# Attention probabilities turned by VectorE and a round trip through HBM in three of four key groups, on one Trainium2 core

## The chip, the core and the metric

The kernel runs on one core of a Trainium2 chip. A core has five engines with a queue of instructions each: TensorE (PE) multiplies matrices, VectorE (DVE) and ScalarE (ACT) work on elements, GpSimd (POOL) does a little arithmetic and issues some of the transfers, SyncE (SP) issues the rest. Each engine takes its instructions strictly in order; semaphores hold an instruction until what it needs is done. Working memory (SBUF) and the accumulators of the matrix engine (PSUM) have 128 partitions each. Data and weights lie in HBM and are moved by 16 DMA engines that all queues share.

The metric is the device time of one execution in microseconds (us); smaller is better. All data is float32.

## The reference

One sequence of 256 tokens goes through one Mamba-2 layer and one layer of sliding-window attention; both add to the residual stream and normalise. The change lies in the attention layer alone: 32 query heads of width 64 share 4 key and value heads, so 8 query heads belong to one key group. A query sees the 128 latest keys, and a sink per head takes part in the softmax.

```
s = einsum("bcqhrd,bckhd->bchrqk", qb, kk) * (hd ** -0.5)
s = where((diff >= 0) & (diff < WINDOW) & (kpos >= 0), s, -inf)
m = maximum(max(s, axis=-1), sk)
p = exp(s - m)
p = p / (sum(p, axis=-1) + exp(sk - m))
o = einsum("bchrqk,bckhd->bcqhrd", p, vv)
o = o * silu(gate)
return o @ w_out
```

Queries lie on the partitions when the softmax is taken over keys. The product with the values contracts over keys, so the keys must then lie on the partitions: the probabilities have to be turned in between.

## The kernel before

**Weights.** All weights stream in once, in units of 128 x 2048. Each half of a unit (512 KB) is loaded by SP (L152), cast by ScalarE to a high part `wh` (L161), and VectorE takes the low part `wl` as the difference (L164). Every product is the sum of three matmuls, high by high, low by high and high by low. A unit keeps TensorE busy for some 5.5 us. Units are split two ahead of the one in use (`AHEAD`), in four buffers each for `wh` and `wl`.

**The attention layer** runs in the order of `B_ORDER`: for the four key groups j, a block of queries ("q", four units, L973), of gates ("g", four units, L249) and of the output projection ("o", four units, L320 to L322), as q0 g0 q1 g1 o0 q2 g2 o1 q3 g3 o2 o3. After each unit `tick()` counts down a list of delayed steps; `later(n, step)` puts a step n units ahead. So the small steps of attention stand between the units of the large products. A scheduler then orders the instructions within each engine's queue by its own estimate; what it made of both kernels is shown below.

**Attention of one group** has two passes, h = 0 for the first 128 queries and h = 1 for the second. `attend(j, h)`: scores on TensorE (L1090, L1097) into the PSUM tiles `ax` (there are four of them, which all small steps share); masks by VectorE into `p` (L1104, L1114); maximum (L1121); exponentials on ScalarE, a head at a time (L1127); scaling by the reciprocal of the sum (L1132). `turn_p`, three or four units later: eight transposes of 128 x 128 on TensorE (L1140; each shows as an instruction of its own), and copies out of PSUM into `pt` (L1149, L1151), which for h = 1 also multiply by the two masks that part the keys of the own block and the block before (L1144). `pv`: product with the values (L1161 for h = 0; L1178 and L1185 for h = 1), gating by VectorE into `o` (L1164, L1191), and the split of `o` into `oH` (ScalarE, L1200) and `oL` (VectorE, L1201), which the projection "o" of that group reads. The turns of the queries (`qtr`, L1051) take two `ax` tiles per group one unit after the block "q".

**Queues.** POOL's queue holds, in this stage, the loads of bias rows (L948), of rows for the residual (L1020), and at its end three normalisations.

Of the kernel before, what the change touches and what calls it, by code (L numbers as in the profile page):

```python
# [8 lines left out]
F32 = mybir.dt.float32  # L9
# [8 lines left out]
P = 128  # L18
# [41 lines left out]
NPT = 6  # L60
# [21 lines left out]
def trunk(ctx: ExitStack, tc: tile.TileContext, A: dict, out: bass.AP, dbg=None):  # L82
# [816 lines left out]
    def turn_x1(h, c, tp, tag, bufs):  # L899
# [8 lines left out]
        x1 = tp.tile([P, 512], F32, tag=tag, name=nm("x1"), bufs=bufs)[:].rearrange("p (k t) -> p k t", k=4)  # L908
# [37 lines left out]
    def bias_row(src):  # L946
        t = bp.tile([P, 512], F32, tag="bias", name=nm("bias"), bufs=2)
        nc.gpsimd.dma_start(t[:], src.partition_broadcast(P))  # L948
        return t
# [34 lines left out]
    for h in range(2):  # L984
        ps = mm_tile()
        for ui in range(4):
# [6 lines left out]
            if h == 0:  # L993
                for c in ((), (), (0, 1, 2, 3), ())[ui]:
                    turn_x1(1, c, bp, "pt", NPT)
# [80 lines left out]
    def attend(j, h):  # L1076


        nk = P * (h + 1)
        q2 = qT[j, h]  # L1080
        p = bp.tile([P, 8, P], F32, tag=f"p{h}", name=nm("p"), bufs=1)
        per = 512 // nk
        for b in range(0, 4, per):
# [17 lines left out]
            for par in range(2):  # L1101
                v = p[:, par * 4 + b : par * 4 + b + per, :]
                if h == 0:
                    nc.vector.tensor_tensor(  # L1104
                        v, pss[par][:].rearrange("p (a k) -> p a k", a=per),
                        mask_a0.unsqueeze(1).to_broadcast([P, per, P]), ALU.add,
                    )
                    continue
                got = pss[par][:].rearrange("p (a k) -> p a k", a=per)

                nc.scalar.copy(v, got[:, :, 64:192])
                for part, m, at in ((0, mask_own, 192), (1, mask_a0[:, 64:], 0)):
                    qs = slice(64 * part, 64 * part + 64)
                    nc.vector.copy_predicated(  # L1114
                        v[qs, :, qs], m[qs].bitcast(U32).unsqueeze(1).to_broadcast([64, per, 64]),
                        got[qs, :, at : at + 64],
# [4 lines left out]
        nc.vector.tensor_reduce(mx, p[:], AX.X, ALU.max)  # L1121
# [4 lines left out]
        for r in range(8):  # L1126
            nc.scalar.activation(  # L1127
                p[:, r, :], p[:, r, :], AF.Exp, bias=ng[:, r : r + 1], accum_out=rs[:, r : r + 1]
# [3 lines left out]
        nc.vector.tensor_tensor(p[:], p[:], ri.unsqueeze(2).to_broadcast([P, 8, P]), ALU.mult)  # L1132

        pts = {}

        def turn_p():
            for par in range(2):
                pt = ax_tile() if h else mm_tile()
                for a in range(4):
                    nc.tensor.transpose(pt[:, a * P : (a + 1) * P], p[:, par * 4 + a, :], ident)  # L1140
                for kc in range(h + 1):
                    t = bp.tile([P, 512], F32, tag="pt", name=nm("pt"), bufs=NPT)
                    if h:
                        nc.vector.tensor_tensor(  # L1144
                            t[:].rearrange("p (a q) -> p a q", a=4), pt[:].rearrange("p (a q) -> p a q", a=4),
# [257 lines left out]
```

## Time and profile before

| what | value |
|---|---|
| median of 3 runs | 993.49 us (993.34 to 993.56) |
| the profiled execution's own time | 993.77 us |
| its span, first to last instruction | 991.8 us |
| TensorE busy | 985.8 us (99%) |
| VectorE busy | 775.2 us (78%) |
| ScalarE busy | 566.5 us (57%) |
| GpSimd busy | 105.4 us (11%) |
| granted TensorE clock | 1.0 |
| first scores of attention (L1090) | at 720.6 us of the span |

A row of the timeline reads: start in us from the beginning of the span, busy time, engine, line, instruction, out<-in, shapes, how many instructions were merged into the row, and in brackets how long the engine had idled before it and what released it. TensorE is pipelined: an instruction's busy time is its time from entry to end, and the next one enters long before that end. What an instruction takes from TensorE's time is therefore the distance from its start to the start of the next row, not its busy time. A row of the view of waits reads: waiting instruction <- what it waited for: us in total, how many times, the longest. In the view of groups the columns behind the bar are the busy time in total, and the mean in ns of one instruction.

### The profile page before, as it was taken

To read this page: it belongs to the slowest core of one execution; us is meant where nothing else is said; L and a number is where in the kernel's file an instruction comes from. 1 tells how busy PE (TensorE), PEld (TensorE's weight loads), DVE (VectorE), ACT (ScalarE), POOL (GpSimd) and SP (SyncE) were. 2 spreads that over 40 slices of the span, in tenths; PEclk is the share of its full clock that TensorE was granted. 3 is DMA by queue.
4 is the path that set the end of the run, shared out by engine and by line. 5 is a ranking of instruction groups with operands and counts; after the bars stand their busy time and mean duration, and the time that the engine had idled before them with its cause. 6 is when DMAs were issued, how large, how long until landed. Compare 5 with 4: busy or idle time off the path is not lost.

```text
span 991.8 us, 18106 instructions
## 1 busy us (share of the span) xinstructions
PE 985.8 (99%) x7132; PEld 897.4 (90%) x7132; DVE 775.2 (78%) x1206; ACT 566.5 (57%) x992; POOL 105.4 (11%) x130
## 2 busy tenths in 40 slices
PE   9999999999999999999999999999999999999997
PEld 8999989999999998999999999888998978978976
DVE  7888897877786887686787687889688786686696
ACT  7585866547646654664664664566455544544542
POOL 0000303004003002100300300303100000000003
PEclk9999999999999999999999999999999999999999
DMA  9688577575576666656657466456754646456432
GB/s 363 241 270 328 164 262 223 172 236 176 193 232 187 219 207 196 208 180 209 208 170 236 139 203 215 157 178 223 253 185 154 192 159 197 158 159 196 158 128 86
DMA packets 61557, 198.90 MB, mean 201 GB/s; under 512 B 6848, under 2 KB 11360, under 8 KB 61216
## 3 DMA queue, kind: packets, MB, share of 16 engines
q1 hardware_dynamic: 58528, 188.53, 57.8%
q0 software_dynamic: 2336, 8.69, 2.7%
q8 instruction: 56, 0.92, 0.4%
q10 hardware_dynamic: 608, 0.52, 0.2%
q14 instruction: 29, 0.24, 0.1%
HBM read 195.49 MB, written 2.23 MB: 199 GB/s over the span
## 4 chain that ended last, share of the span: by engine, by line
PE 99%; DVE 0%; DVEq 0%; issue 0%
PE mm L249 53%; PE mm L973 11%; PE mm L320 9%; PE mm L321 9%; PE mm L322 9%; PE ax L628 2%; PE ax L604 1%; PE ax L1097 1%; PE ax L1090 0%; PE ax L587 0%; PE mm L387 0%; PE ax L1161 0%; PE ax L1140 0%; PE ax L1051 0%; PE ax L1178 0%; PE mm L1140 0%
## 5 line engine op out<-in xcount | busy, mean ns | idle before, releaser
L164 DVE TENSOR_TENSOR wl<-wr,wh 128x1024 fp32r<-128x1024 f32 (+2 forms) x338 | 393.1, 1182 | 103.6 <-ACT wh L161 101.5
L161 ACT ACTIVATE wh<-wr 128x1024 fp32r<-128x1024 f32 (+2 forms) x338 | 332.1, 1010 | 193.4 <-issue 69.1
L249 PE MATMUL mm<-xH,wh 128*128 128x256 f32 x1280 | 355.4, 278 | 0.0
L249 PE MATMUL mm<-xL,wh 128*128 128x256 f32 x1280 | 354.0, 277 | 0.0
L249 PE MATMUL mm<-xH,wl 128*128 128x256 f32 x1280 | 353.9, 277 | 0.0
L249 PEld LDWEIGHTS mm<-xH,wh 128*128 128x128 f32 x1280 | 240.4, 188 | 1.9 <-issue 0.5
L249 PEld LDWEIGHTS mm<-xL,wh 128*128 128x128 f32 x1280 | 240.6, 188 | 1.0
L249 PEld LDWEIGHTS mm<-xH,wl 128*128 128x128 f32 x1280 | 240.5, 188 | 0.2 <-DVE wl L164 0.2
L320 PE MATMUL mm<-wh,yH 128*128 128x512 f32 x256 | 101.4, 396 | 0.0
L321 PE MATMUL mm<-wh,yL 128*128 128x512 f32 x256 | 99.8, 390 | 0.0
L322 PE MATMUL mm<-wl,yH 128*128 128x512 f32 x256 | 99.7, 389 | 0.0
L644 POOL TENSOR_TENSOR yz<-yz,z 128x256 f32<-128x256 f32 x32 | 32.8, 1033 | 468.9 <-DVE yz L639 468.9
L249 PE MATMUL mm<-x1H,wh 128*128 128x256 f32 x256 | 71.7, 280 | 0.0
L491 DVE SCALAR_TENSOR_TENSOR cv<-mm,pc,cv 128x255 f32<-128x255 f32 x144 | 68.6, 477 | 3.3 <-ACT cv L489 1.9
L249 PE MATMUL mm<-x1L,wh 128*128 128x256 f32 x256 | 70.8, 277 | 0.0
L249 PE MATMUL mm<-x1H,wl 128*128 128x256 f32 x256 | 70.8, 276 | 0.0
L973 PE MATMUL mm<-wh,x1H 128*128 128x512 f32 x160 | 62.9, 393 | 0.0
L973 PE MATMUL mm<-wl,x1H 128*128 128x512 f32 x160 | 61.8, 389 | 0.0
L973 PE MATMUL mm<-wh,x1L 128*128 128x512 f32 x160 | 60.9, 389 | 0.0
L320 PEld LDWEIGHTS mm<-wh,yH 128*128 128x128 f32 x256 | 48.1, 188 | 10.3 <-DVE z L580 0.9
L322 PEld LDWEIGHTS mm<-wl,yH 128*128 128x128 f32 x256 | 48.0, 188 | 10.2
L321 PEld LDWEIGHTS mm<-wh,yL 128*128 128x128 f32 x256 | 48.1, 188 | 9.0
(226 smaller groups left out, 1346.8 us busy)
## 6 DMA issues: line engine op xcount, KB each, us to landing
wr<-in_wa SPq DMA_DIRECT2D x154, 512.0 KB, 5.0
wr<-in_wo SPq DMA_DIRECT2D x64, 512.0 KB, 4.4
wr<-in_wq SPq DMA_DIRECT2D x32, 512.0 KB, 4.5
wr<-in_wg SPq DMA_DIRECT2D x31, 512.0 KB, 4.7
wr<-in_wb SPq DMA_DIRECT2D x16, 512.0 KB, 4.1
wr<-in_wb SPq DMA_DIRECT2D x32, 256.0 KB, 3.7
rb<-rscr SPq DMA_DIRECT2D x11, 512.0 KB, 4.1
wr<-in_wkv SPq DMA_DIRECT2D x8, 512.0 KB, 4.9
```

Of the source, the lines that this page charges most:

```text
L161: m = nc.scalar.activation(h[:, sl], v, AF.Copy)
L164: m = nc.vector.tensor_tensor(l[:, sl], v, h[:, sl].bitcast(F32), ALU.subtract)
L249: m = nc.tensor.matmul(ps, a, b, start=first and i == 0, stop=last and i == 2)
L320: pinned(nc.tensor.matmul(ps, aH[:, k, hs], u.h[:, ks], start=k == 0 and add is None, stop=False), pin)
L321: pinned(nc.tensor.matmul(ps, aL[:, k, hs], u.h[:, ks], start=False, stop=False), pin)
L322: pinned(nc.tensor.matmul(ps, aH[:, k, hs], u.l[:, ks], start=False, stop=k == 3), pin)
L491: nc.vector.scalar_tensor_tensor(a[:, sft:], ps[:, : S - sft], w(3 - sft), a[:, sft:], ALU.mult, ALU.add)
L604: nc.tensor.transpose(ps[:, o : o + P], st.xs[i][:, c * P : (c + 1) * P], ident)
L628: nc.tensor.matmul(ps[64 * r : 64 * r + 64, cols], xd[:, c, r, :], e[:, 256:] if c else e[:, :256], start=c == 0, stop=c == 1,)
L644: nc.gpsimd.tensor_tensor(v, v, st.z[i][:], ALU.mult)
L973: m = nc.tensor.matmul(ps[:], (x1H, x1L, x1H)[i][:, kk, hs], (u.h, u.h, u.l)[i][:, ks], start=(kk, i) == (0, 0), stop=ui == 3 and (k, i) = ...
L1097: nc.tensor.matmul(pss[par][qs, at : at + 192], q2[rows, b + i, qs], kT[rows, j, 64 * part : 64 * part + 192], start=True, stop=True,)
```

## The change

In the groups j = 0, 1 and 2 (`far`) TensorE no longer turns the probabilities. `p` is laid out with the 32-wide blocks of keys outermost. VectorE transposes each block of 32 x 32 in place in the grid (one instruction over 128 x 1024, into a tile `z`), POOL stores `z` to HBM (512 KB), and when that has landed four more transfers (128 KB each, in runs of 1 KB) bring the blocks back to the partitions where they belong, into `pt`. For h = 1 VectorE multiplies by the two masks five units later, now in two instructions of 128 x 1024 from SBUF. The product with the values comes later: nine units after the first pass's `attend` in group 0 and eleven in the groups 1 and 2, and the two passes' products fall on the same unit. The group j = 3 still turns on TensorE.

Around it: the factor 0.5 goes from the gating into one more instruction on the reciprocals (128 x 8) in all groups; `o` shares the two buffers of the queries before their turn (tag "qt"); `p` and `z` share three buffers; `pt` has three buffers of 1024 for six of 512; the bias rows have one buffer for two; the tiles of the LayerNorm at both ends of the layer follow the new sizes.

```diff
@@ def attend(j, h):
-        p = bp.tile([P, 8, P], F32, tag=f"p{h}", name=nm("p"), bufs=1)
+        p = bp.tile([P, 1024], F32, tag="p", name=nm("p"), bufs=3)
+        far = j < 3
+        byhead = p[:].rearrange("p (c r b) -> p r c b" if far else "p (r c b) -> p r c b", r=8, c=4)
...
-        nc.vector.tensor_tensor(p[:], p[:], ri.unsqueeze(2).to_broadcast([P, 8, P]), ALU.mult)
+        nc.vector.tensor_scalar(ri, ri, 0.5, None, ALU.mult)
+        nc.vector.tensor_tensor(
+            byhead, byhead, ri.unsqueeze(2).unsqueeze(3).to_broadcast([P, 8, 4, 32]), ALU.mult
+        )
...
+        def turn_far():
+
+            z = bp.tile([P, 1024], F32, tag="p", name=nm("z"), bufs=3)
+            nc.vector.transpose(z[:], p[:])
+            zd = dram.tile([P, 1024], F32, tag="zd", name=nm("zd"), bufs=2)
+            nc.gpsimd.dma_start(zd[:], z[:])
+            t = pt_tile(0)
+            for c in range(4):
+                nc.gpsimd.dma_start(
+                    pts[0][32 * c : 32 * c + 32].rearrange("b i r a -> b i (r a)"),
+                    zd[:, c * 256 : (c + 1) * 256].rearrange("(i b) f -> b i f", b=32),
+                )
+
+            def parts():
+                own = pt_tile(1)
+                nc.vector.tensor_tensor(own, t, masked(1, 8), ALU.mult)
+                nc.vector.tensor_tensor(t, t, masked(0, 8), ALU.mult)
+
+            if h:
+                later(5, parts)
...
-            o = bp.tile([P, 4, P], F32, tag="o", name=nm("o"), bufs=1)
+            o = bp.tile([P, 4, P], F32, tag="qt", name=nm("o"), bufs=2)
...
-                nc.vector.scalar_tensor_tensor(
-                    o[:], ov[:].rearrange("p (a t) -> p a t", a=4), 0.5, sg[j][:, :, hs], ALU.mult, ALU.mult
-                )
+                gated(ov[:], 0, P)
...
-        last = j == 3
-        later(4 if last and h == 0 else 3, turn_p)
-        later((5 if last else 6) if h == 0 else (8 if 0 < j < 3 else 4), pv)
+        if not far:
+            later(3 + (h == 0), turn_p)
+            later(5 - h, pv)
+        else:
+            turn_far()
+            later((11 if j else 9) - 3 * h, pv)
         if h == 0:
-            later(1 if last else 3, lambda: attend(j, 1))
+            later(1 if j == 3 else 3, lambda: attend(j, 1))
```

**TensorE, group 1, at the end of the first unit of gates of group 2.** Before, this is what stood between that unit and the next: the product of the second pass with the values (`vt`), then the two turns of the queries `qt`, each into an `ax` tile of its own.

```order
L1178 MATMUL ax_9494<-pt_9256,vt 64x256
L1178 MATMUL ax_9494<-pt_9265,vt 64x256
L1178 MATMUL ax_9495<-pt_9258,vt 64x256
L1178 MATMUL ax_9495<-pt_9267,vt 64x256
L1185 MATMUL ax_9494<-pt_9258,vt 64x256
L1185 MATMUL ax_9495<-pt_9256,vt 64x256
L1185 MATMUL ax_9494<-pt_9267,vt 64x256
L1185 MATMUL ax_9495<-pt_9265,vt 64x256
L1051 MATMUL ax_9508<-cc,qt_9413 128x128 x4
L1051 MATMUL ax_9515<-cc,qt_9422 128x128 x4
```

Now, at the same place, both passes' products stand there (L1216 for the first, L1230 and L1237 for the second), and the second turn of the queries comes six matmuls of the next unit (L248) later.

```order
L1216 MATMUL ax_9467<-pt_8872,vt 64x512 x2
L1230 MATMUL ax_9474<-pt_9118,vt 64x256 x2
L1230 MATMUL ax_9475<-pt_9309,vt 64x256 x2
L1237 MATMUL ax_9474<-pt_9309,vt 64x256
L1237 MATMUL ax_9475<-pt_9118,vt 64x256
...
L1052 MATMUL ax_9488<-cc,qt_9384 128x128 x4
L248 MATMUL mm_9516<-x1H,wh_9348 128x256
...
L248 MATMUL mm_9516<-x1H,wl_9349 128x256
L1052 MATMUL ax_9495<-cc,qt_9393 128x128 x4
```

Five `ax` tiles are asked for in a row where there are four: `ax_9495` takes the place of `ax_9467`, once VectorE has read that. Group 2 has the same rows.

**VectorE, group 0, the second pass.** Before, the stretch from the product of the first pass (`o_8673`) to the next unit's split held the copies out of PSUM; L164 is the split of weights.

```order
L1164 SCALAR_TENSOR_TENSOR o_8673<-ax_8674,sg_8156 128x512
L1144 TENSOR_TENSOR pt_8687<-ax_8682,cc 128x512
L1144 TENSOR_TENSOR pt_8689<-ax_8682,cc 128x512
L1201 TENSOR_TENSOR oL_8679<-o_8673,oH_8678 128x4x128
L1144 TENSOR_TENSOR pt_8696<-ax_8691,cc 128x512
L1144 TENSOR_TENSOR pt_8698<-ax_8691,cc 128x512
```

Now the masks (L1168, L1169) stand one unit later between the halves of a split, and wait for the four loads of `pt_8556`.

```order
L163 TENSOR_TENSOR wl_8774<-wr_8777,wh_8773 128x1024
L163 TENSOR_TENSOR wl_8880<-wr_8881,wh_8879 128x1024
L1168 TENSOR_TENSOR pt_8834<-pt_8556,cc 128x8x4x32
L1073 SCALAR_TENSOR_TENSOR sg_8695<-sg_8695,mm_8708 128x256
L1169 TENSOR_TENSOR pt_8556<-pt_8556,cc 128x8x4x32
L163 TENSOR_TENSOR wl_8880<-wr_8883,wh_8879 128x1024
L163 TENSOR_TENSOR wl_8965<-wr_8966,wh_8964 128x1024
```

The gating and the split of `o` have left this stretch: they stand behind the softmax of group 1 now, as the next rows show.

```order
L1204 TENSOR_TENSOR o_8940<-ax_8941,sg_8154 128x512
...
L1245 TENSOR_TENSOR oL_8939<-o_8940,oH_8938 128x4x128
L1139 TENSOR_TENSOR p_8837<-p_8837,sm_8850 128x8x4x32
L1204 TENSOR_TENSOR o_8947<-ax_8948,sg_8154 128x4x64
L1156 STREAM_TRANSPOSE z_8868<-p_8837 128x1024
L1204 TENSOR_TENSOR o_8947<-ax_8949,sg_8154 128x4x64
L1073 SCALAR_TENSOR_TENSOR sg_8695<-sg_8695,mm_8889 128x256
L163 TENSOR_TENSOR wl_9026<-wr_9027,wh_9025 128x1024
L1245 TENSOR_TENSOR oL_8939<-o_8947,oH_8938 128x4x128
```

The last row (`oL` of the second pass) is what the second half of the first output unit of group 0 reads.

**POOL, group 0.** Before, only small loads stood in this part of the queue; now it reads as follows.

```order
L947 DMA bias_8459<-in_qb 128x512
L1158 DMA zd_8326<-z_8324 128x1024
L1161 DMA pt_8328<-zd_8326 32x4x256 x4
L1021 DMA gb_1062_8633<-in_lng 128x512
L1021 DMA gb_1063_8635<-in_lnb 128x512
L1158 DMA zd_8554<-z_8552 128x1024
L1161 DMA pt_8556<-zd_8554 32x4x256 x4
L947 DMA bias_9239<-in_qb 128x512
```

The last two loads for the residual (`gb`) now stand behind the first pass's round trip, and the queries' bias of group 1 ahead of it.

More of the change, by code (lines that the diff above doesn't have):

```diff
@@ L946, in bias_row @@
     def bias_row(src):
-        t = bp.tile([P, 512], F32, tag="bias", name=nm("bias"), bufs=2)
+        t = bp.tile([P, 512], F32, tag="bias", name=nm("bias"), bufs=1)
         nc.gpsimd.dma_start(t[:], src.partition_broadcast(P))
@@ L1178, in pv @@
                         nc.tensor.matmul(
-                            ovs[part][64 * par : 64 * par + 64], vt[:, part, vs], pt_of(part, par, whole, part),
+                            into(part, par), vt[:, part, vs], pt_of(part, par, whole, 2 * part, 2 * part + 2),
                             start=True, stop=False,
```

102 lines of the change are left out of this document (58 added, 44 removed).

## The prediction

> **What bounds the kernel now.** I read the page first (busy times, slices, the chain that ended last), then the view of waits for the attention layer (690 to 960 us), then TensorE's timeline around the instructions that go.
>
> ```profile
> PE 985.8 (99%) x7132; PEld 897.4 (90%) x7132; DVE 775.2 (78%) x1206; ACT 566.5 (57%) x992; POOL 105.4 (11%) x130
> PEclk9999999999999999999999999999999999999999
> PE 99%; DVE 0%; DVEq 0%; issue 0%
> ```
>
> TensorE is the whole chain, at the full granted clock. So an instruction taken from its queue is worth its pitch (start to next start), unless a new wait on that queue eats it.
>
> ```profile
> DVE wl L164 <- ACT wh L161: 33.0, 20, 4.2
> PEld ax L1140 <- ACT wh L161: 2.4, 3, 0.8
> PEld ax L1161 <- issue: 1.4, 4, 0.4
> PEld ax L1051 <- issue: 1.2, 3, 0.4
> ```
>
> In 270 us of attention nothing holds TensorE's queue for more than 0.8 us at a time, and VectorE still has waits of its own; DVE and ACT are cover, not bound.
>
> **1. The transposes that go.** Six groups of eight, of these the first and the last after a block of weights and the first and the last after a product with the values, each with the row behind it:
>
> ```profile
> 738.22 1.04 PE L1140 MATMUL mm<-cc,p 128*128 128x128 f32 x8
> 739.19 1.53 PE L1097 MATMUL ax<-kT,qT 64*64 64x192 f32 x32
> ...
> 758.22 1.09 PE L1140 MATMUL ax<-cc,p 128*128 128x128 f32 x8
> 759.07 0.37 PE L249 MATMUL mm<-x1H,wh 128*128 128x256 f32 x1
> ...
> 864.37 1.03 PE L1140 MATMUL mm<-cc,p 128*128 128x128 f32 x8
> 865.33 0.88 PE L1097 MATMUL ax<-kT,qT 64*64 64x192 f32 x16
> ...
> 884.36 1.09 PE L1140 MATMUL ax<-cc,p 128*128 128x128 f32 x8
> 885.21 0.49 PE L973 MATMUL mm<-wh,x1H 128*128 128x512 f32 x1
> ```
>
> Start to next start they take 0.97, 0.85, 0.96 and 0.85 us; group 1 is like group 2. Sum 0.97 + 2 x 0.96 + 3 x 0.85 = 5.44 us off TensorE. [...]
>
> **2. Both products on one unit.** Group 3 has the form that the groups 0 to 2 get; before, those have the products apart.
>
> ```profile
> 952.75 1.08 PE L1161 MATMUL ax<-pt,vt 128*64 128x512 f32 x4
> 953.66 1.03 PE L1178 MATMUL ax<-pt,vt 128*64 128x256 f32 x8
> 954.62 0.66 PE L1185 MATMUL ax<-pt,vt 64*64 64x256 f32 x8
> 955.21 0.50 PE L320 MATMUL mm<-wh,oH 128*128 128x512 f32 x1
> ...
> 809.06 0.39 PE L322 MATMUL mm<-wl,oH 128*128 128x512 f32 x1
> 809.38 1.08 PE L1161 MATMUL ax<-pt,vt 128*64 128x512 f32 x4
> 810.39 1.09 PE L1140 MATMUL ax<-cc,p 128*128 128x128 f32 x8
> ...
> 838.48 0.28 PE L249 MATMUL mm<-x1H,wl 128*128 128x256 f32 x1
> 838.69 1.08 PE L1178 MATMUL ax<-pt,vt 128*64 128x256 f32 x8
> 840.30 1.09 PE L1051 MATMUL ax<-cc,qt 128*128 128x128 f32 x8
> 841.14 0.36 PE L249 MATMUL mm<-x1H,wh 128*128 128x256 f32 x1
> 841.34 0.28 PE L249 MATMUL mm<-x1L,wh 128*128 128x256 f32 x1
> ```
>
> Together 955.21 - 952.75 = 2.46; apart 1.01 + 1.61 = 2.62; and the separate entry at 809.06 cost 0.32 for a pitch of 0.23. Saved: 3 x (0.16 + 0.09) = 0.75 us. Against it, in the groups 1 and 2 the second turn of the queries gets an entry and an exit of its own, 0.21 + 0.20 for two pitches of 0.12: 2 x 0.17 = 0.35 us back. TensorE's work so falls by 5.44 + 0.75 - 0.35 = 5.85 us.
>
> **3. A new wait, in the groups 1 and 2.** After the change the second turn of the queries needs the `ax` tile of the first product, and so VectorE's gating; the gating writes into a buffer of "qt" and so needs the first turn done. Before, VectorE and ScalarE do this at that place:
>
> ```profile
> 838.68 1.06 ACT L161 ACTIVATE wh<-wr 128x1024 fp32r<-128x1024 f32 x1 [3.41 <-PE mm L249]
> 839.91 1.05 ACT L161 ACTIVATE wh<-wr 128x1024 fp32r<-128x1024 f32 x1
> 839.77 1.23 DVE L164 TENSOR_TENSOR wl<-wr,wh 128x1024 fp32r<-128x1024 f32 x1 [2.59 <-ACT wh L161]
> 840.91 0.75 DVE L1191 SCALAR_TENSOR_TENSOR o<-ax,sg 128x256 f32<-128x256 f32 x2
> ```
>
> Count from T, the start of the products (838.69 here). VectorE: half a split at T + 1.08 (1.14 to the next row), the gate's 0.33, the other half of the split, ahead of the gating in the new order, then the gating of 128 x 512 (0.68, as L1164's like): begun at 1.08 + 1.14 + 0.33 + 1.14 = T + 3.69, done at T + 4.4. TensorE: products 2.46, half of 0.84 for the first turn, six matmuls at 0.12 with an exit 0.9: T + 3.8. It waits 0.7 us with the hand-over. Bounds: 0, if the gating goes ahead of the half split; 0.7 + 1.14 = 1.8, if one more half split stands ahead. I take 0.7, since the order and the rows give it: 1.4 us in both. Behind that wait stand 42 matmuls of a unit; VectorE for its part waits in the second gating for that turn, with a split queued behind, but units are split two ahead, some 10 us.
>
> **4. VectorE, ScalarE and the 32 x 32 transposes.** No row shows that instruction. Nearest below is a pass over the same tile, 1.22 us; above, two such passes, 2.44.
>
> ```profile
> L1132 DVE TENSOR_TENSOR p<-p,sm 128x1024 f32<-128x1024 f32 x8 | 9.8, 1219 | 0.1
> L1144 DVE TENSOR_TENSOR pt<-ax,cc 128x512 f32<-128x512 f32 x16 | 10.1, 680 | 0.0
> ```
>
> I take 1.22 (one pass in, one out, like L1132). Per group two transposes (2.4), two masks from SBUF at 1.22 for four at 0.68 (-0.3), a copy less (-0.7; and one less on ScalarE), the small factor twice (0.3): some +1.8 us on VectorE per 74 us, free under a TensorE that is the bound. The laying out of `p` in blocks I cost at nothing; its cover is VectorE's idle time. [...]
>
> **5. The round trip, and group 0.** Nearest rows for a store and a load from POOL, with POOL's time for issuing one:
>
> ```profile
> rb<-rscr POOLq DMA_DIRECT2D x5, 512.0 KB, 7.6
> el<-rscr POOLq DMA_DIRECT2D x2, 256.0 KB, 3.6
> DMA to landing us min/median/max: 3.4/5.3/8.8
> L1020 POOL DMA_DIRECT2D gb<-in_lnb x4: 536/538/538, 663.7 to 739.9; - x4
> L1003 POOL COPY kd<-kd x2: 1414/4014/6613, 679.3 to 688.7; 128x256 f32<-128x256 f32 x2
> ```
>
> (The row of landings is that of `rb`.) Store 5 us, then four issues of 0.54 of which three lie ahead of the last load, and 4 to 5 us for that: about 11 us. Bounds: 3.4 + 1.6 + 3.4 = 8.4, and 8.8 + 1.6 + 8.8 = 19.2 us. In the groups 1 and 2 some 15 us lie between the transpose and the masks (two and a half units of gates and queries), in all groups more than that before the products. Group 0 is the tight one:
>
> ```profile
> 751.62 1.22 DVE L1132 TENSOR_TENSOR p<-p,sm 128x1024 f32<-128x1024 f32 x1
> 764.71 1.06 ACT L161 ACTIVATE wh<-wr 128x1024 fp32r<-128x1024 f32 x1 [2.33 <-PE mm L249]
> 784.92 0.40 PE L320 MATMUL mm<-wh,oH 128*128 128x512 f32 x1
> ```
>
> The scaling ends 0.8 us earlier than here (852.84 less 100: 752.0; the turn of 0.97 ahead of it is gone), half a split follows, then the transpose: 754.2. VectorE reaches the masks behind a half split whose cast waits for TensorE (764.71, now 2.9 us earlier) and at the end of its own backlog: 765.1. That leaves 10.9 us, as much as the trip takes. From there VectorE runs masks, splits, the softmax of group 1, both gatings and one transpose to `oL` of the second pass at about 785.0; TensorE, 2.1 us earlier than before, begins the output unit at 782.8 and asks for that `oL` half a unit later, at 785.5. A lateness of the loads beyond 0.5 us is paid in full; I put 0.3 us for it.
>
> **The sum.** 5.85 - 1.4 - 0.3 = 4.15 us off. The profiled execution took 993.77 us, 0.28 above the median of the runs; it would take 989.6, and the median 993.49 goes to 989.3. I say 989.4 us. The tail (group 3) is costed at nothing: its transposes keep their places, and the two small factors (0.17 each, as L1123's like) lie under TensorE's units.
>
> **The rivals.** A difference under 0.2% (2 us) cannot be told from no change here.
>
> *No new wait.* VectorE gets to the gating before the half split, or the fifth tile is free: 993.49 - 5.85 = 987.6. For it: no wait of TensorE above 0.8 us now. Against: the order puts the split ahead. Chance 0.22.
>
> *Late in group 0.* The trip takes some 14 us (512 KB at 7.6, loads at 5): 3 us beyond the margin, all on TensorE: 992.3, no difference that can be told. For it: the `rb` row; weights share the DMA engines. Against: the rows of 256 KB. With the transposes at 2.44 us it is half as bad. Chance 0.17.
>
> *Slower: POOL's transfers are starved.* The masks stand in VectorE's queue in front of the splits. A trip of 19.2 us (the upper bound) is 8.3 us over the 10.9, of which 0.5 are free, 7.8 fall on TensorE in group 0, and about 4 over the 15 us in the groups 1 and 2, which VectorE's idle time there takes up: 993.49 - 4.45 + 7.8 = 996.8. It decides from a trip of 18 us on. For it: a POOL copy of the same shape took 1.4 us and 6.6 us, so something can hold POOL while VectorE works. Against: eight issues of the residual's rows, in the same traffic, took 536 to 538 ns each. [...] Chance 0.12.
>
> **How the numbers follow.** My forecast has 0.45, and 0.04 remain for what I have not seen. Faster by over 0.2% (under 991.5): 0.45 + 0.22 + 0.05 of the late case and the rest = 0.72; within: 0.16; slower: 0.12. The forecast's own range is 988.4 to 990.6 (its waits halved or doubled). The range for 8 in 10 runs from 987.3 (no wait) to 993.0 (late in group 0).
>
> **What would show it.** Right: TensorE's chain still 99%, 16 rows of transposes instead of 64, the two turns of the queries 0.7 us apart from waiting, VectorE's masks in group 0 with a wait of 0 to 1 us for the loads, the transposes at 1.2 us. Wrong: waits of TensorE at the first output unit of group 0, waits of VectorE for loads above 3 us, POOL issues much over 0.54 us, or block-wise passes over `p` well above 1.22 us.

## The result, and the profile after

| | before | after |
|---|---|---|
| median of 14 runs | 993.48 us (992.77 to 994.35) | 993.87 us (991.60 to 995.06) |
| ratio of after to before | | 1.0001, 95% interval 0.9993 to 1.0010 |
| the profiled execution | 993.77 us, span 991.8 | 995.06 us, span 992.9 |
| keys' turn to the tail (below) | 285.98 us | 286.95 us |

No difference that can be told, where 989.4 was forecast. The profiled execution of after is the slowest of its 14, so the trace shows somewhat more loss than the median has.

The page after: busy times, and the chain that ended last.

```profile
PE 982.9 (99%) x7084; PEld 893.7 (90%) x7084; DVE 780.8 (79%) x1211; ACT 565.1 (57%) x989; POOL 122.8 (12%) x160
PE 87%; DMA 5%; DVE 4%; ACT 1%; issue 1%; POOL 0%; ACTq 0%; SPq 0%; DVEq 0%; POOLq 0%
```

The 48 transposes are gone (7132 to 7084 instructions), but the chain is no longer TensorE alone: 5% transfers and 4% VectorE stand in it. TensorE's timeline shows where it loses time in the attention layer.

```profile
697.53 1.03 PE L1009 MATMUL ax<-cc,kd 128*128 128x128 f32 x8
...
762.29 0.60 PE L1052 MATMUL ax<-cc,qt 128*128 128x128 f32 x4
764.34 0.63 PE L1052 MATMUL ax<-cc,qt 128*128 128x128 f32 x4 [1.45 <-DVE qt L962]
764.72 0.36 PE L248 MATMUL mm<-x1H,wh 128*128 128x256 f32 x1
...
785.36 0.50 PE L319 MATMUL mm<-wh,oH 128*128 128x512 f32 x1
786.09 0.50 PE L320 MATMUL mm<-wh,oL 128*128 128x512 f32 x1 [0.23 <-DVE oL L1245]
...
788.52 0.40 PE L321 MATMUL mm<-wl,oH 128*128 128x512 f32 x1
789.68 0.50 PE L319 MATMUL mm<-wh,oH 128*128 128x512 f32 x1 [0.76 <-ACT oH L1244]
791.08 0.50 PE L320 MATMUL mm<-wh,oL 128*128 128x512 f32 x1 [0.90 <-DVE oL L1245]
...
794.13 0.63 PE L320 MATMUL mm<-wh,oL 128*128 128x512 f32 x1
794.56 0.63 PE L321 MATMUL mm<-wl,oH 128*128 128x512 f32 x1
795.12 1.76 PE L1103 MATMUL ax<-kT,qT 64*64 64x192 f32 x32
...
843.47 0.36 PE L248 MATMUL mm<-x1H,wh 128*128 128x256 f32 x1
...
844.40 0.66 PE L1052 MATMUL ax<-cc,qt 128*128 128x128 f32 x4
...
984.48 0.81 PE L1318 MATMUL ax<-gb,cc 128*128 128x256 f32 x3
```

The first and the last row bound the stretch in which the change lies: from the turn of the keys to the first matmul of the tail, 984.48 - 697.53 = 286.95 us. Before, the same two matmuls start at 696.96 and 982.94: 285.98. The opening ahead of it, which the change hardly touches, varies from one profiled run to the next (695.8 to 698.5 us over all kernels below), so I compare traces by this stretch and whole times by medians.

Two places of group 0 lose time. The turns of the queries of the next group (762.29 to 764.72) take 2.44 us instead of 0.85, since the second waits for VectorE. The first output unit (785.36 to 795.12) takes 9.76 us; before, it took 5.47. Three times it waits: for `oL` of the first pass, for `oH` and for `oL` of the second, some 0.4 + 0.9 + 1.1 us beyond the usual pitch. Then its last matmuls stand 0.43 us apart instead of 0.23. The windows (us, then busy time and instructions of PE, PEld, DVE, ACT and POOL, granted clock, DMA share, GB/s) show the clock:

```profile
785.00:790.00 5.00, 3.97 (x16) 2.47 (x15) 4.95 (x9) 3.48 (x6) 0.56 (x1) 1.00 0.00 2
790.00:797.00 7.00, 6.10 (x45) 4.15 (x45) 7.00 (x9) 3.94 (x6) 2.20 (x4) 0.76 0.85 256
```

VectorE is busy through both windows (11.95 of 12 us; in the kernel before it was 11.16), and in the second the granted clock falls to 0.76 (1.00 in the kernel before). By the pitches, the low clock costs some 1.3 us in this unit and 0.23 in the scores behind it.

What stands behind the late `oL` is on VectorE's timeline and on POOL's.

```profile
750.95 0.69 DVE L1023 TENSOR_TENSOR xr<-xr,gb 128x512 f32<-128x512 f32 x1 [3.00 <-DMA gb<-in_lng]
...
755.16 1.24 DVE L1156 STREAM_TRANSPOSE z<-p 128x1024 f32<-128x1024 f32 x1
...
772.43 1.23 DVE L1168 TENSOR_TENSOR pt<-pt,cc 128x1024 f32<-128x1024 f32 x1 [4.96 <-DMA pt<-zd]
...
784.82 0.17 DVE L1136 TENSOR_TENSOR sm<-sm 128x8 f32<-128x8 f32 x1 [2.55 <-ACT p L1133]
...
790.34 0.68 DVE L1245 TENSOR_TENSOR oL<-o,oH 128x512 fp32r<-128x512 f32 x1
```

```profile
756.69 0.54 POOL L1158 DMA_DIRECT2D zd<-z  x1 [10.39 <-DVE z L1156]
763.10 2.20 POOL L1161 DMA_DIRECT2D pt<-zd  x4 [5.87 <-DMA zd<-z]
```

The residual's rows `gb` wait for loads that were issued behind the first pass's trip. The transpose of the second pass ends at 756.40 (755.16 + 1.24), the masks start at 772.43: a trip of 16.0 us. For 4.96 of them VectorE stands at the masks, with splits, softmax, gating and `oL` queued behind. On the way to `oL` it also waits 2.55 us for ScalarE's exponentials of group 1, which themselves could start only behind the masks. The last `oL` is done at 791.0.

The balance over the stretch, from the two timelines: transposes off TensorE -5.44; products on one unit -0.45 (2.47 for 2.62 in three groups); turns of the queries in two halves -0.06; the last group's transposes +0.08; entries and exits around the halved turns and elsewhere +0.82; second query turn of group 0 +1.59; first output unit +4.29; scores behind it +0.23. Sum +1.06, against 286.95 - 285.98 = +0.97.

### The profile page after: what moved, and what is told of

Its sections match the earlier page's. It is cut to its first block, busy times and chain, and to the rows that moved or that the text cites. A ratio compares the mean times of both kernels' runs of the same rounds, so it can differ in the third digit from the quotient of the medians.

```text
span 992.9 us, 18078 instructions
## 1 busy us (share of the span) xinstructions
PE 982.9 (99%) x7084; PEld 893.7 (90%) x7084; DVE 780.8 (79%) x1211; ACT 565.1 (57%) x989; POOL 122.8 (12%) x160
## 4 chain that ended last, share of the span: by engine, by line
PE 87%; DMA 5%; DVE 4%; ACT 1%; issue 1%; POOL 0%; ACTq 0%; SPq 0%; DVEq 0%; POOLq 0%
PE mm L248 46%; PE mm L319 9%; PE mm L320 9%; PE mm L972 9%; PE mm L321 9%; PE ax L627 2%; DMA zd<-z 1%; DVE wl L163 1%; DMA wr<-in_wa 1%; DMA xr<-in_first 1%; DMA rb<-rscr 1%; DMA pt<-zd 1%; PE ax L603 1%; DMA gb<-in_lng 1%; PE ax L1103 0%
## 5 line engine op out<-in xcount | busy, mean ns | idle before, releaser
L248 PE MATMUL mm<-xH,wh 128*128 128x256 f32 x1280 | 355.2, 277 | 0.2 <-ACT wh L194 0.2
L248 PE MATMUL mm<-xH,wl 128*128 128x256 f32 x1280 | 354.0, 277 | 1.0 <-DVE wl L163 1.0
L248 PE MATMUL mm<-xL,wh 128*128 128x256 f32 x1280 | 354.0, 277 | 0.0
L248 PEld LDWEIGHTS mm<-xH,wh 128*128 128x128 f32 x1280 | 240.5, 188 | 1.9 <-issue 0.5
L248 PEld LDWEIGHTS mm<-xH,wl 128*128 128x128 f32 x1280 | 240.3, 188 | 1.2 <-DVE wl L163 1.2
L248 PEld LDWEIGHTS mm<-xL,wh 128*128 128x128 f32 x1280 | 240.4, 188 | 1.0
L248 PE MATMUL mm<-x1H,wh 128*128 128x256 f32 x256 | 72.0, 281 | 0.0
L248 PE MATMUL mm<-x1H,wl 128*128 128x256 f32 x256 | 70.9, 277 | 0.0
L248 PE MATMUL mm<-x1L,wh 128*128 128x256 f32 x256 | 70.9, 277 | 0.0
L328 DVE SCALAR_TENSOR_TENSOR xr<-mm,r,xr 128x512 f32<-128x512 f32 x64 | 47.2, 746 | 11.7 <-PE mm L321 7.3
```

The source lines that it names most:

```text
L248: m = nc.tensor.matmul(ps, a, b, start=first and i == 0, stop=last and i == 2)
L328: nc.vector.scalar_tensor_tensor(v, ps, rms[:, h : h + 1], v, ALU.mult, ALU.add)
```

## The experiments

My theory was that all of the loss lies in group 0 and goes through VectorE's queue: first the residual rows that wait for loads behind the first pass's trip, then the masks that wait for the second pass's. Rivals: the trips' traffic harms everything; VectorE is simply fuller; GpSimd's queue starves. The times, with the two places of group 0 and the stretch from each profile:

| kernel | median us | ratio to before, 95% | stretch | second query turns | first output unit |
|---|---|---|---|---|---|
| before | 993.48 | | 285.98 | 0.85 | 5.47 |
| after | 993.87 | 1.0001 (0.9993, 1.0010) | 286.95 | 2.44 | 9.76 |
| group 0 on TensorE | 992.06 | 0.9985 (0.9976, 0.9994) | 284.08 | 0.79 + 0.83 waiting | 5.56 |
| residual early | 996.67 | 1.0027 (1.0016, 1.0038) | 285.81 | 0.79 | 6.85 |
| loads of group 0 free | 989.98 | 0.9968 (0.9956, 0.9980) | 281.95 | 1.38 | 5.56 |
| trips on SyncE | 989.44 | 0.9964 (0.9952, 0.9976) | 282.44 | 2.54 | 5.56 |
| SyncE, residual late | 990.47 | 0.9961 (0.9947, 0.9975) | 282.51 | 1.10 | 7.07 |
| residual late | 994.40 | 1.0011 (1.0002, 1.0020) | 287.24 | 1.12 | 0.40 waiting + 10.02 |
| all on TensorE | 995.35 | 1.0019 (1.0010, 1.0027) | 288.10 | 0.76 + 1.45 waiting | 5.47 |
| all on TensorE, own `o` | 994.19 | 1.0003 (0.9994, 1.0013) | 286.31 | 0.85 | 5.47 |
| one turn more through HBM | 991.18 | 0.9977 (0.9968, 0.9986) | 283.47 | 1.10 | 7.71 |
| masks on GpSimd | 992.07 | 0.9982 (0.9970, 0.9994) | 283.27 | 0.26 waiting + 2.53 | 5.99 |
| SyncE, residual late, masks on GpSimd | 988.45 | 0.9955 (0.9942, 0.9968) | 281.06 | 1.13 | 5.56 |
| trips on ScalarE | 991.97 (one run) | | 285.23 | 1.02 | 2.12 waiting + 7.75 |

The ratios, not the medians, compare kernels here, since each kernel was timed beside the kernel before in its own session.

### Which group loses: group 0 on TensorE

```diff
-        far = j < 3
+        far = 0 < j < 3
...
-            later(3 + (h == 0), turn_p)
-            later(5 - h, pv)
+            later(3 + (h == 0 and j == 3), turn_p)
+            later(5 - h if j == 3 else 6 - 2 * h, pv)
```

> Group 0 is turned on TensorE again, at the units it had in the kernel before; groups 1 and 2 keep the round trip. Theory (the whole loss lies in group 0: the residual rows queue behind the first pass's round trip and make its second query turn 1.65 us longer, and the masks that wait for the second pass's loads make the first output unit 4.29 us longer): that unit takes its 5.47 us again, and the four groups of eight transposes of groups 1 and 2 (0.91 us each) are still saved, so about 990.0 us, 3.5 under the kernel before. Rival 1 (the round trips slow the weights' loads and VectorE everywhere): groups 1 and 2 lose what their transposes save, about 993.5. Rival 2 (VectorE's longer passes alone, not the wait): between, 991 to 992.

992.06: faster than before, but 2 us short of the theory. The first output unit is whole again (5.56). Of what is missing, 0.8 us sits at the second query turn, which waits 0.83 us; the next experiment shows that this is another part of the change. Part of the rest is the 0.82 of entries and exits in the balance above, which this expectation left out. The groups 1 and 2 keep their gain, so the first rival (loss everywhere) falls. The time alone is also that of the rival "VectorE is fuller" (991 to 992); it does not tell the two apart.

### What the rest of the change costs: all groups on TensorE, and an own buffer for `o`

```diff
-        far = j < 3
+        far = False
...
-            later(3 + (h == 0), turn_p)
-            later(5 - h, pv)
+            later(3 + (h == 0 and j == 3), turn_p)
+            later(5 - h if j == 3 else 6 + 2 * h if h and j else 6 - 2 * h, pv)
```

> All groups are turned on TensorE, at the units of the kernel before: no trip at all, and what is left of the change is the rest (merged products, one probabilities tile of three buffers, the output rows in the query rows' two buffers, one bias buffer). The prediction's terms for this rest come to 0.4 us less than before: 993.1. With group 0 alone on TensorE the second query turn of group 0 lost 1.5 us, as the query rows came behind the output rows on VectorE; if this holds wherever the products stand near a query turn, 994.5 to 998.

995.35: the rest alone makes the kernel 1.9 us slower. VectorE's timeline of this kernel, and the turn that waits:

```profile
759.36 0.69 DVE L1204 TENSOR_TENSOR o<-ax,sg 128x512 f32<-128x512 f32 x1
...
762.97 1.28 DVE L1046 TENSOR_TENSOR qt<-mm,bias 128x512 f32<-128x512 f32 x2
```

```profile
768.48 0.63 PE L1052 MATMUL ax<-cc,qt 128*128 128x128 f32 x4 [1.19 <-DVE qt L962]
```

The query rows (`qt`) stand behind the output rows (`o`, `oL`), with which they share two buffers. Then `o` got one of its own, the probabilities giving up one:

```diff
-            p = bp.tile([P, 1024], F32, tag="p", name=nm("p"), bufs=3)
+            p = bp.tile([P, 1024], F32, tag="p", name=nm("p"), bufs=2)
...
-            o = bp.tile([P, 4, P], F32, tag="qt", name=nm("o"), bufs=2)
+            o = bp.tile([P, 4, P], F32, tag="o", name=nm("o"), bufs=1)
```

> All groups on TensorE as in the kernel without trips that took 1.9 us more than before, but the output rows have a buffer of their own again (the probabilities have two buffers instead of three to make room). Theory (those 1.9 us, and with them the part of the gain that group 0 on TensorE did not show, are the query rows of group 1 standing behind the output rows on VectorE, since both share two buffers): the second query turn of group 0 takes 0.8 to 0.9 us in one piece, 993.1 to 993.7. Rival (block layout, merged masks or the single bias buffer cost it): 995 still.

994.19, 1.0003 of before: the turns take 0.85 us in one piece, and most of the 1.9 us is gone. So the sharing costs as long as the products stand just ahead of a query turn; the changed kernel has moved group 0's products away from there and does not pay for it, the kernel with group 0 on TensorE does. The kernel with all groups on TensorE (288.10) and the one with trips in the groups 1 and 2 (284.08) lie 4.0 us apart; 0.6 of that is the shorter wait at the query turn. The other 3.4 are at least what the terms give for two groups: transposes 2 x (0.96 + 0.85), products 0.30, less 0.82 for entries and exits, 3.1 us. So the trips of the groups 1 and 2 cost TensorE nothing that shows.

### The wait for the trip: loads of group 0 that wait for no store

```diff
+            free = A["wkv"][0]
...
-                    zd[:, c * 256 : (c + 1) * 256].rearrange("(i b) f -> b i f", b=32),
+                    (zd if j else free)[:, c * 256 : (c + 1) * 256].rearrange("(i b) f -> b i f", b=32),
```

> In group 0 alone the eight loads read 1 KB runs of a weight array instead of the stored probabilities, so that they wait for no store; the stores, the loads and all passes stay, and group 0's probabilities are not the right ones. Theory: VectorE does not wait at the masks of group 0, the first output unit takes 5.5 to 6.0 us instead of 9.76 with the clock at full, about 989.5 us. Rival 1 (the loads' traffic itself, or VectorE's work, makes the first output unit late): it keeps 8 us or more, 992.5 or above. Rival 2 (the residual rows are all of it): the query turn is 0.79 us, and the output unit stays as it was, 992.

989.98, the output unit 5.56, the mean granted clock of the profiled execution 1.0: as the theory has it. But with nothing to wait for, the scheduler put these loads and the masks far ahead (issued between 664 and 682 us), so the run takes away the wait, the traffic and two passes of VectorE at once.

### The residual rows: early, late

```diff
-RES_AT = [1, 2, 3, 4, 9, 10, 11, 12]
+RES_AT = [1, 2, 3, 4, 5, 6, 7, 8]
```

> The residual rows of the last two chunks are loaded and applied four units earlier, so that none of their loads stands in the GpSimd queue behind a store or loads of the round trip. Theory: the second query turn of group 0 takes 0.79 us instead of 2.44, VectorE does not wait for gb, the second pass's transpose is done about 2 us earlier, and the waits of the first output unit shrink by about that: 990 to 991.5 us, if the clock does not fall there, 992 if it does. Rival 1 (the trip alone is the matter, wherever the residual rows stand): the first output unit still takes 9.8 us and the gain is only the 1.65 us of the query turn, 992.2.

Slower, 996.67. The second query turn is 0.79 us, but VectorE now waits 2.98 us for `gb` (until 713.29) ahead of the query rows of group 0, and the second of their two turns comes late:

```profile
715.68 0.60 PE L1052 MATMUL ax<-cc,qt 128*128 128x128 f32 x4
718.23 1.02 PE L1052 MATMUL ax<-cc,qt 128*128 128x128 f32 x4 [1.95 <-DVE qt L962]
```

```profile
719.00:721.00 2.00, 2.00 (x12) 2.00 (x11) 1.97 (x4) 1.71 (x2) 0.60 (x2) 0.50 0.87 256
```

One wait of 1.95 us, and behind it the clock at half. The stretch of the table starts ahead of this turn, so it counts the loss; the median is 2 us above the profiled execution (994.56), which one trace can't explain. The first output unit still lost 1.4 us, less than the 4.3 of the changed kernel; but TensorE also came to it 2.1 us later, counted from the turn of the keys, which gave VectorE that much more time.

```diff
-RES_AT = [1, 2, 3, 4, 9, 10, 11, 12]
+RES_AT = [1, 2, 3, 4, 9, 10, 14, 15]
```

> The same later place for the last residual rows, with the trips on GpSimd as in the changed kernel. Theory (the first output unit is late because GpSimd's trip takes 15.9 us where SyncE's took 11.4): the second query turn is 0.8 to 1.3 us, the second trip still takes 14 to 16 us, VectorE still waits 3 to 5 us at the masks, and the first output unit stays at 7 to 9.8 us: 991 to 992.5. Rival (the residual rows behind the first trip are the root of both): the first output unit takes 5.5 to 6 us as well, 988 to 989.5.

994.40. The query turn falls to 1.12 us, so that loss did hang on the residual rows. The output unit stays at 10.02, with the trip as long as it was (the masks wait for 5.06 us):

```profile
771.55 1.23 DVE L1168 TENSOR_TENSOR pt<-pt,cc 128x1024 f32<-128x1024 f32 x1 [5.06 <-DMA pt<-zd]
```

VectorE no longer waits for `gb`, and its transpose ends 1.1 us earlier (755.31). The masks start 0.9 us earlier, and two of the moved residual passes, 1.3 us, now stand between them and `oL` and take that back. So the rows behind the first trip are worth about 1 us there and are not the root of the late output unit: that part of my theory falls.

### The queue of the trip: SyncE, and ScalarE

```diff
-            nc.gpsimd.dma_start(zd[:], z[:])
+            nc.sync.dma_start(zd[:], z[:])
...
-                nc.gpsimd.dma_start(
+                nc.sync.dma_start(
                     pts[0][32 * c : 32 * c + 32].rearrange("b i r a -> b i (r a)"),
```

> The store and the four loads of each trip are issued by SyncE in the weights' queue instead of by GpSimd. If the long trip (15.9 us in group 0's second pass, stores of 5.8 us and loads of 6 to 7.5 us) belongs to GpSimd's software queue, the store lands in about 3 us and the loads in about 4.5, as the weights' loads do, and the trip takes about 9 us; if it belongs to the traffic, it stays at 14 to 16 us. The time is open: the residual rows no longer stand behind the trip (1.65 us less), but weights' loads now stand behind a store that waits for VectorE: 989.5 to 991 us if they still come in time, 995 or more if TensorE has to wait for weights.

> The trips are issued by ScalarE, on a queue of its own: neither GpSimd's nor the one that the weights stand in. Only the landing times are asked for, since ScalarE stands at the store and the loads until they may go. If the second trip of group 0 was long on GpSimd (store 5.8 us, loads 6 to 8 us) because of GpSimd's queue, its store lands in 3 to 4.4 us and the loads in about 4 to 5, as on SyncE's; if it was long because the weights' loads go on beside it, which they do not where both stand in one queue, the loads take 6 to 8 us here too. Time: ScalarE's wait of 5 to 10 us a trip comes to 995 to 1015 us.

The second of them has `nc.scalar` in the same two places. On SyncE 989.44, 0.36% faster than before: TensorE loses nothing at the first output unit, and VectorE comes to the masks without a wait (no bracket in the row); the second query turn waits 1.55 us, like the 1.45 of the changed kernel. On ScalarE 991.97 in one run.

```profile
767.44 1.22 DVE L1168 TENSOR_TENSOR pt<-pt,cc 128x1024 f32<-128x1024 f32 x1
```

The transfers in the window 750 to 775 us, with KB each and the median us to landing, in the changed kernel, on SyncE and on ScalarE:

```profile
zd<-z POOLq DMA_DIRECT2D x1, 512.0 KB, 5.8
pt<-zd POOLq DMA_DIRECT2D x4, 128.0 KB, 7.2
```

```profile
zd<-z SPq DMA_DIRECT2D x1, 512.0 KB, 4.4
pt<-zd SPq DMA_DIRECT2D x4, 128.0 KB, 4.1
```

```profile
zd<-z ACTq DMA_DIRECT2D x1, 512.0 KB, 4.4
pt<-zd ACTq DMA_DIRECT2D x4, 128.0 KB, 7.8
```

On ScalarE's queue the loads are as slow as on GpSimd's. So GpSimd's queue is not what makes the loads slow. The store is 1.4 us slower there than on either; but in the kernel whose loads wait for no store, GpSimd's store of the same size landed in 3.6 us, with one load of weights beside it where the changed kernel has three:

```profile
zd<-z POOLq DMA_DIRECT2D x1, 512.0 KB, 3.6
```

So the slower store need not be the queue's doing either. What differs on SyncE is what it does not issue meanwhile; its timeline with the trips on SyncE, and in the changed kernel:

```profile
756.15 0.33 SPq L1158 DMA_DIRECT2D zd<-z  x1
760.53 1.75 SPq L1161 DMA_DIRECT2D pt<-zd  x4
762.38 5.50 SPq L151 DMA_DIRECT2D wr<-in_wb  x6
```

```profile
755.27 12.55 SPq L151 DMA_DIRECT2D wr<-in_wb  x7
```

From the store to the last of the trip's loads, no weights are asked for on SyncE; the next six follow behind. With the trip on another queue, loads of 512 KB run beside all of it. In the kernel after this (SyncE, residual late) two loads of weights stand just ahead of the trip's in SyncE's queue, and there these took 6.9 us:

```profile
756.28 1.53 SPq L151 DMA_DIRECT2D wr<-in_wb  x2
759.67 1.79 SPq L1161 DMA_DIRECT2D pt<-zd  x4
```

```profile
pt<-zd SPq DMA_DIRECT2D x4, 128.0 KB, 6.9
```

The landings go with where the weights stand: 6.9 to 7.8 us beside or behind them, 4.1 us ahead of them. That it is the traffic is argued from these kernels; no run changed the traffic alone.

### Whose time is it: SyncE with the residual late, and masks on GpSimd

```diff
-RES_AT = [1, 2, 3, 4, 9, 10, 11, 12]
+RES_AT = [1, 2, 3, 4, 9, 10, 14, 15]
...
-            nc.gpsimd.dma_start(zd[:], z[:])
+            nc.sync.dma_start(zd[:], z[:])
...
-                nc.gpsimd.dma_start(
+                nc.sync.dma_start(
                     pts[0][32 * c : 32 * c + 32].rearrange("b i r a -> b i (r a)"),
```

> The trips stay on SyncE's queue, and the residual rows of the last chunk are applied in units 14 and 15 instead of 11 and 12, so that VectorE has them behind the query rows of the second group. With the trips on SyncE the second query turn of group 0 still took 2.54 us instead of 0.79. Theory (TensorE now comes to this turn 4 us earlier, since the attention work that stood ahead of it is gone or moved, and VectorE has four residual passes and the transpose ahead of the query rows): 0.8 to 1.2 us there, 987.5 to 988.3 in all. Rival (weight splits fill the freed place, and VectorE is late anyway): 2.3 us or more there, 989.4.

990.47, and the same stretch as without the late residual (282.51 and 282.44). The query turn gets its 1.4 us back, and the output unit loses 1.5:

```profile
784.53 0.50 PE L320 MATMUL mm<-wh,oL 128*128 128x512 f32 x1 [0.42 <-DVE oL L1245]
...
788.06 0.50 PE L320 MATMUL mm<-wh,oL 128*128 128x512 f32 x1 [0.51 <-DVE oL L1245]
```

Two of the moved residual passes came to lie ahead of `oL`. But the trip, slower in this kernel, holds VectorE as well:

```profile
768.43 1.23 DVE L1168 TENSOR_TENSOR pt<-pt,cc 128x1024 f32<-128x1024 f32 x1 [1.76 <-DMA pt<-zd]
```

So this run does not tell a full queue of VectorE from a late trip. Two experiments take the masks out of that queue, and with them the wait for the trip, the first from the changed kernel, the second from the kernel just shown:

```diff
-                nc.vector.tensor_tensor(own, t, masked(1, 8), ALU.mult)
-                nc.vector.tensor_tensor(t, t, masked(0, 8), ALU.mult)
+                nc.gpsimd.tensor_tensor(own, t, masked(1, 8), ALU.mult)
+                nc.gpsimd.tensor_tensor(t, t, masked(0, 8), ALU.mult)
```

> The changed kernel with its two mask passes on GpSimd, which has nothing else to do there; the trips stay on GpSimd, and VectorE's other instructions keep their order. Theory (the long trip reaches TensorE only because VectorE, in order, stands 5 us at the masks with the weight splits, the gating and oL of the first output unit behind them): the trip stays at about 16 us, but the first output unit takes 5.5 to 7 us instead of 9.76 with the clock at full, the second query turn of group 0 stays at 2.4: 989.5 to 991. By the passes of 128x512 that GpSimd has at 1.3 us each, the two passes end at about 777.5, and the products of the second pass may wait for them by up to 1 us. Rival (the traffic of the trip, not VectorE's wait, delays the weights of the output units): no gain, 993 or above.

> Trips on SyncE, the last residual rows late, and the mask passes on GpSimd. With the first two alone the second query turn fell from 2.54 to 1.10 us and the first output unit rose from 5.5 to 7.07. Theory (in group 0 VectorE's own queue is the bound up to oL, so that what it no longer does ahead of the one it owes to the other): without its 2.4 us of masks and 1.8 us of wait both are gone, the query turn 1.1 us and the output unit 5.5, 1.6 us under the kernel without GpSimd's masks: 987.5 to 988.8. Rival (the output unit is late for another reason, such as ScalarE's exponentials ahead of the gating): 7 us still, 989.5 to 990.5.

In the changed kernel with this edit alone the trip is as long as ever, and it is now GpSimd that waits for it:

```profile
771.19 2.97 POOL L1168 TENSOR_TENSOR pt<-pt,cc 128x1024 f32<-128x1024 f32 x1 [6.08 <-DMA pt<-zd]
774.24 2.40 POOL L1169 TENSOR_TENSOR pt<-pt,cc 128x1024 f32<-128x1024 f32 x1
```

The first output unit takes 5.99 us instead of 9.76. The passes themselves are not what made it late: with the trips on SyncE they stay on VectorE, and the unit takes 5.56. So this shows the mechanism: a long trip reaches TensorE because VectorE stands at the masks, with `oL` in order behind them. VectorE does not get the passes off for free, though. A split of weights that ran beside the second of them took 3.24 us, where the longest in the changed kernel took 1.76:

```profile
774.47 3.24 DVE L163 TENSOR_TENSOR wl<-wr,wh 128x1024 fp32r<-128x1024 f32 x1
```

The median is 992.07, too. Five of its twelve runs lie at 988.65 to 990.28, the profiled one (989.96) among them, the others at 991.93 to 996.23. The masks end at 776.64, and TensorE already waits 0.28 us for them ahead of the second pass's products. So no room is left here, and a longer trip would fall on TensorE directly; whether that is what the slower runs did stays open, since no trace of one was taken.

With the trips on SyncE and the residual late as well, 988.45: ratio 0.9955, and the stretch is 1.45 us shorter than without GpSimd's masks, as expected. The output unit takes 5.56 us, and the two query turns stand in one row, 1.13 us to the next. Since the edit takes away both the passes and the wait of 1.76 us, it does not say how much each was worth. This kernel beats before and after. It is not the limit of the idea: of the 5.85 us forecast to leave TensorE, 4.92 (285.98 - 281.06) are kept.

### One turn more through HBM

To the kernel with SyncE and late residual:

```diff
-        far = j < 3
+        far = j < 3 or h == 0
...
-            later((11 if j else 9) - 3 * h, pv)
+            later(5 if j == 3 else (11 if j else 9) - 3 * h, pv)
```

> Trips on SyncE, residual rows late, and the first pass of the last group goes through HBM too, so that eight transposes more leave TensorE (0.92 us of the pair 0.92 and 0.82). Theory: its trip of 11 to 12 us ends before its products, 27 us later, and hides: 0.9 us under the same kernel without it, 986.5 to 987.5. Rival (the last group's products or the output units come late): equal to it or slower, 988 to 990.

991.18, no gain: the way of the rival, though above its 988 to 990. The 0.92 us of transposes went, the other pass's transposes waited 1.22 us instead, and the first output unit took 7.71 us instead of 7.07:

```profile
943.59 1.07 PE L1179 MATMUL ax<-cc,p 128*128 128x128 f32 x8 [1.22 <-DVE p L1139]
```

## Why the prediction was wrong

**Right: the transposes (term 1). Too high: the net of term 2.** The 5.44 us of transposes went as forecast. The merged products saved 0.45 us, not 0.75, and entries and exits cost 0.82 us, not 0.35. With the small terms of the balance this makes 5.05 us off TensorE, ahead of all waits, where 5.85 was forecast. The two kernels that differ only in the groups 1 and 2 bear out the part of those groups (3.4 us, where these terms give 3.1). Of the 0.82, the second halves of the query turns explain 0.24 a group: 0.93 us between 843.47 and 844.40, of which six matmuls take 0.69. The rest lies elsewhere and was not traced.

**Wrong: the wait of term 3.** It did not come, though VectorE kept the forecast's time: the gating begins at 844.28, which is T + 3.69 from the start of the products at 840.59, and its first instruction takes 0.68 us.

```profile
844.28 1.57 DVE L1204 TENSOR_TENSOR o<-ax,sg 128x512 f32<-128x512 f32 x3
```

```profile
844.40 0.42 PEld L1052 LDWEIGHTS ax<-cc,qt 128*128 128x128 f32 x4 [0.18 <-ACT qT L1056]
```

The second turn starts at 844.40, before the gating is done. What it waited for, 0.18 us, was ScalarE's copy of the first turn (`qT`). In group 2 the same rows stand at 916.56 and 916.68. So the turn did not wait for VectorE to read the first product, as the change's description and the prediction have it. This is the case "the fifth tile is free" that the rival "No new wait" names. The forecast's 5.85 less 1.4, 4.45, comes near the 5.05 only because the two errors partly cancel: that is luck.

**Right: the price of the transpose (term 4).**

```profile
L1156 DVE STREAM_TRANSPOSE z<-p 128x1024 f32<-128x1024 f32 x6 | 7.4, 1238 | 0.0
```

1.24 us, like one pass over the tile (1.22 before) and not like two, the upper bound of 2.44. What was wrong in this term is "free under a TensorE that is the bound", and with it a term put at nothing, the second query turn of group 0. VectorE is covered on average (79% busy), not in group 0: TensorE comes to the second query turn 4.0 us earlier (762.29, before 766.32), because the attention work ahead of it is gone or moved, while VectorE has its rows ready only 2.2 us earlier (764.19, before 766.38). With the trips on SyncE, where the wait for `gb` was shorter (0.62 and 0.52 us), that turn still took 2.54 us. I had taken TensorE's gain at this place without asking who would be late next. It cost 1.59 us.

**The step that failed: term 5.** "That leaves 10.9 us, as much as the trip takes ... I put 0.3 us for it." The trip took 16.0 us. VectorE started the masks at 772.43 instead of 765.1: 0.6 from the later opening, 1.6 from the transpose (1.1 of them the residual rows and their wait, as the run with the residual late shows), 5.1 from the trip. The last `oL` came at 791.0 instead of 785.0. TensorE paid 4.29 + 0.23 us where the term said 0.3, some 1.5 of them in lowered clock, which the prediction has nowhere. I had put store and loads at 5 and 4 to 5 us; they took 5.8 and 7.2, with seven loads of weights beside them.

**The rivals.** "Late in group 0" (17 in 100) was what happened, and the landings speak for the traffic of weights that it names (the trip's loads 7.2 us beside them, 4.1 us ahead of them on SyncE). It was 3 us over the margin there and 5 here, and it lacked the clock and the query turn. "Starved POOL transfers" had a longer trip, but not for its reason: the issues of the trip's loads took 550 to 572 ns (536 to 538 for the small loads before), ScalarE's loads were as slow (7.8 us), and GpSimd's store was fast beside little traffic (3.6 us). In the kernel before, VectorE was at work beside POOL's copy of 1.41 us (from 679.28) as beside the one of 6.61 (from 688.73), so these rows leave open what held the longer one. "No new wait" was right for the groups 1 and 2.

**What would show it** did show it: waits of TensorE at the first output unit of group 0 and a wait of VectorE for loads above 3 us stood in the list as signs of a wrong prediction.

**Slips in the recorded sums.** "852.84 less 100: 752.0" should read 751.62 + 1.22 = 752.84, less 0.8. The upper end of the forecast's own range, with its waits doubled, is 993.49 - (5.85 - 3.4) = 991.0, not 990.6. Neither changes what was forecast.

## What to carry to other kernels

A margin has to be counted on the engine that will wait in order, at the place where it will wait, and once more after the change has made the other engine earlier: here the 1.8 us of transposes taken from TensorE in group 0 came back as 6.1 us of waits and lowered clock. The loads of the same round trip through HBM landed in 4.1 us ahead of the weights in the weights' own queue, and in 7.2 or 7.8 us beside them from another: the price of a trip has to be taken from rows with the same traffic beside them. And a wait for a transfer belongs on an engine that has nothing queued behind it: with the masks, and their wait of 6.08 us, on GpSimd, the first output unit took 5.99 us instead of 9.76.

## What the runs showed that I had not expected

- **The clock.** In the changed kernel three waits within 6 us (2.4 us beyond the pitch) were followed by some 3 us at a lowered clock; with the residual early one wait of 1.95 us was followed by 0.50 in the window 719 to 721 us, and with the trips on ScalarE one of 2.12 us by 0.61 and 0.54 in the windows 785 to 787 and 787 to 789 us. Single waits of 1.45 us (changed kernel, query turn) and 1.55 (on SyncE) were followed by none. Waits and lowered clock together took 4.5 us in the changed kernel, 2.4 of them the waits, and 3.8 with the residual early, 2.1 of them the wait beyond the pitch. What lowers the clock was not shown.
- **GpSimd as a place for passes.** Two mask passes of 128x1024 took 2.97 and 2.40 us there, against 1.23 on VectorE. They cost TensorE 0.28 us of waiting, and VectorE's split beside the second took 3.24 us, where the longest in the changed kernel took 1.76.
- **A shared buffer as an order.** `o` in the query rows' two buffers put some 1.8 us on TensorE's stretch (288.10 against 286.31) with no instruction added, by what it made VectorE do first.
